# Adding the experts' rows to two DRAM buffers in turn, with a third buffer for results

## Chip, cores and metric

One core of a Trainium2 chip. The metric is the device time of one launch, in microseconds; the kernel before takes 2149.32 us (median of 3 runs, 2149.24 to 2149.33).

## What is computed

Two transformer blocks on 512 tokens of width 1024, in float32. The first block ends in a mixture of experts, and the change lies there and in the step behind it:

```python
def moe_ffn(h, ...):
    ...
    def expert_block(acc, blk):
        tok, wts, e = blk
        out = swiglu(h_pad[tok], w_gu[e], w_down[e])
        return acc.at[tok].add(out * wts[:, None].astype(out.dtype)), None
    acc, _ = lax.scan(expert_block, jnp.zeros((N + 1, D), h.dtype), ...)
    return acc[:N] + swiglu(h, w_sh_gu, w_sh_down)
...
        x_lat = x_lat + gt2 * rms_norm(f_lat.reshape(B, T, D), g_post_ffn[l])
```

There are 64 experts of inner width 256; each token goes to 8 of them, and its 8 weighted results are summed. To this comes a shared expert for all tokens. The second block begins with a norm of the sum.

## The kernel before

Everything runs on one core. The program is written in order, with tiles taken from pools; each tile has a tag, and a tag has a number of buffers. Outside stretches marked otherwise, a list scheduler that works at compile time, with its own estimates of each instruction's time, orders the instructions of each engine, and waits on semaphores keep the dependences. With another dependence it can find another order. An engine works through its queue in order, so an instruction that waits holds up everything behind it.

**The expert stage** (`experts`, from L1206 on) goes over groups of one or two experts. For each group it

- gathers the rows of the group's tokens from `h2d` in DRAM (`gather`, on POOL's queue) and turns them with PE (`expert_rows`);
- loads the expert's weights, 3 MB, through SP's queue into `raw` buffers and splits each piece into a high part on ACT (L132, `whi`) and a low part on DVE (L133, `wlo`), so that three products on PE make one in float32;
- forms the first product and the gate (`expert_in`; small blocks pass through a tile `esum`, L1044, with two buffers);
- one group later forms the second product (`expert_out`): ACT scales it into a result tile `ey` of 128 x 1024 (L1071), a tag with two buffers.

The result is then summed into the tokens' rows in two ways. The first 384 columns (`CA`) go through PE: ACT and POOL split them into `eys` (L1084, L1085), DVE makes a one-hot matrix (L1087), and PE adds the product to four accumulators `acc` (L1094). The other 640 columns go through DRAM: `expert_send` (L1075) issues an indirect DMA on POOL's queue that adds the rows to the buffer `cb` in DRAM. Since such an addition reads and writes `cb`, each one waits until the one before it has landed. It also reads `ey`, so a buffer of `ey` comes free only when its addition has landed. `cb` is cleared at the start by four DMAs on SP's queue (L1219). A loop at the end, for experts with more tokens than planned for, sends to `cb` too.

With two parts in a group there are 67 additions. `finish` puts an addition behind the subtraction L1085 of its group (`issue_after`) if that is the group's last expert.

**The combination** (`second_block`, L1435 on) starts when PE has added the shared expert to `acc` and to four more PSUM tiles. SP loads the four tiles of `cb` into `cf` (L1455, L1459) and the four of `x1d` into `cx` (L1456, L1461). Here DVE, ACT and POOL are under `manual_schedule`: they keep the order of the program. `take` copies PSUM to SBUF on ACT (L1469 to L1471); `add` (L1474) adds the two, for tile 0 on DVE and for tiles 1 to 3 on POOL; `squares` (L1477) sums squares on ACT. Tile 0 then goes ahead alone: norm, residual, next norm, turned by PE (L1392) and split again by ACT and DVE. DVE does the `rstd` of tiles 1 to 3 (one call, 128x3) after tile 0's normed row and before tile 0's split:

```python
                for t in range(2, NT):
                    squares(fs[t], ss[:, t:t + 1])
                rs = self.rstd(wp, ss[:, 1:], D)
                self.turn_tile(pp, xn, xs[0], xs[1], 0)
```

Then come the products of the second block, which need the split.

Of the kernel before, what the change touches and what calls it, by code (L numbers as in the profile page):

```python
# [1 line left out]

# [8 lines left out]
F = mybir.dt.float32  # L11
R = mybir.dt.float32r
# [9 lines left out]
T = 512  # L22
# [43 lines left out]
class Kernel:  # L66
# [762 lines left out]
    def order(self, mp, pp):  # L829


        nc, r = self.nc, self.route
        MM, key = r["MM"], r["key"]
        ka, kb, kac, kbc = key[:, 0:64], key[:, 64:128], key[:, 128:129], key[:, 129:130]
        ps = pp.tile([128, 65], F, tag="mm", name="mm", bufs=4)
        for t in range(NT):
            nc.tensor.matmul(ps[:, 0:64], r["ones"], MM[:, t, 0], start=t == 0, stop=t == NT - 1)
        for t in range(NT):
            nc.tensor.matmul(ps[:, 64:65], MM[:, t].rearrange("p a e -> p (a e)"), r["ones"][:, 0:1], start=t == 0, stop=t == NT - 1)
        tl = lambda name, *s: mp.tile([128, *s], F, name=name)  # L840
        v = nc.vector
        row, col, gt, rank = tl("krow", 64), tl("kcol", 1), tl("kgt", 64), tl("krank", 1)
        v.tensor_mul(row, ps[:, 0:64], ka)
        v.tensor_add(row, row, kb)
        v.tensor_scalar(col, ps[:, 64:65], kac, kbc, op0=OP.mult, op1=OP.add)
        v.tensor_scalar(gt, row, col, None, op0=OP.is_gt)
        v.tensor_reduce(rank, gt, axis=X, op=OP.add)
        perm = r["perm"]
        for i in range(2):
            h = slice(64 * i, 64 * i + 64)  # L850
            v.tensor_scalar(perm[h, h], self.iota_f[h, 0:64], rank[h], None, op0=OP.is_equal)

        p2 = pp.tile([128, NT, 128], F, tag="mm", name="tp", bufs=4)
        for t in range(NT):
            nc.tensor.transpose(p2[:, t], r["MW"][:, t].rearrange("p a e -> p (a e)"), self.ident)
        mt = mp.tile([128, D], F, tag="ey", name="kmt", bufs=2)[:, 0:512].rearrange("p (t e) -> p t e", t=NT)
        nc.scalar.activation(mt, p2, AF.Copy)
        ps = pp.tile([128, 64], F, tag="mm", name="mm", bufs=4)
        nc.tensor.matmul(ps, key[0:64, 130:258], perm[0:64, 0:64], start=True, stop=True)
        v.tensor_copy(r["eid"], ps)  # L860
        v.tensor_copy(r["eidi"], r["eid"])
        ps = pp.tile([128, NT, 2, 64], F, tag="mm", name="mm", bufs=4)
        for t in range(NT):
            nc.tensor.matmul(ps[:, t].rearrange("p a e -> p (a e)"), mt[:, t], perm, start=True, stop=True)
        M = mp.tile([128, NT, 64], BF, name="kM")
        v.tensor_copy(M, ps[:, :, 0])
        w = r["MW"][:, :, 1]
        nc.scalar.activation(w, ps[:, :, 1], AF.Copy)
        self.three_parts(v, r["aux"], w)
        self.places(pp, M, r["pos"])  # L870
        ps = pp.tile([128, 64], F, tag="mm", name="mm", bufs=4)
        for t in range(NT):
            nc.tensor.matmul(ps, r["ones"], M[:, t], start=t == 0, stop=t == NT - 1)
        v.tensor_copy(r["cnt"], ps)
# [110 lines left out]
    def expert_rows(self, tiles, pp, xg, parts=((0, 128),)):  # L985


        nc = self.nc
        pool, tags = tiles
        m = parts[-1][1]  # L990
        w = parts[0][1]
        if len(tags) == 2:
            hi, lo = (pool.tile([128, KD, 128], R, tag=tag, name="xT", bufs=2)[:, :, 0:m] for tag in tags)
            cut, out = [(lambda z: z, hi, lo)], [(hi, lo)]
        else:
            x = pool.tile([128, KD, 256], R, tag=tags[0], name="xT", bufs=2)
            if len(parts) == 1:
                at = 128 if w > 64 else w
                hi, lo = x[:, :, 0:w], x[:, :, at:at + w]
                cut, out = [(lambda z: z, hi, lo)], [(hi, lo) if w > 64 else (x[:, :, 0:2 * w],)]  # L1000
            elif w == 64:
                v = x.rearrange("p k (j h w) -> p k h j w", j=2, h=2)
                cut = [(lambda z: z.rearrange("p k (j w) -> p k j w", j=2), v[:, :, 0], v[:, :, 1])]
                out = [(x[:, :, 0:128],), (x[:, :, 128:256],)]
            else:

                cut = [(lambda z: z[:, :, 0:w], x[:, :, 0:w], x[:, :, 256 - w:256]),
                       (lambda z: z[:, :, w:m], x[:, :, w:m], x[:, :, m:256 - w])]
                out = [(x[:, :, 0:w], x[:, :, 256 - w:256]), (x[:, :, w:256 - w],)]
        for u in range(2):  # L1010
            p2 = pp.tile([128, 4, 128], F, tag="mm", name="tp", bufs=4)[:, :, 0:m]
            for k in range(4):
                c = (4 * u + k) * 128
                nc.tensor.transpose(p2[:, k], xg[0:m, c:c + 128], self.ident[0:m, 0:m])
            for some, hi, lo in cut:
                self.split_ps(hi[:, 4 * u:4 * u + 4], lo[:, 4 * u:4 * u + 4], some(p2))
        return out

    def expert_in(self, mp, pp, gu, blocks, between=None):
# [17 lines left out]
        for ps, (xT, a, p0, p1) in zip(pss, blocks):  # L1037
            if len(xT) == 2:
                nc.scalar.activation(a[p0:p1], ps[p0:p1, 0:256], AF.Silu)
                nc.vector.tensor_mul(a[p0:p1], a[p0:p1], ps[p0:p1, 256:512])  # L1040
            else:

                n = p1 - p0
                s = mp.tile([128, 512], F, tag="esum", name="esum", bufs=2)[p0:p1]  # L1044
                nc.scalar.activation(s, ps[n:2 * n], AF.Copy)
                nc.vector.tensor_add(s, ps[0:n], s)  # L1046
                nc.scalar.activation(a[p0:p1], s[:, 0:256], AF.Silu)
                nc.vector.tensor_mul(a[p0:p1], a[p0:p1], s[:, 256:512])
# [74 lines left out]
    def first_block(self):  # L1123

        nc, tc, ins = self.nc, self.tc, self.ins
        dram = lambda name, n, m=D: self.dram.tile([n, m], F, name=name)
        h2d, x1d, cb = dram("h2d", T), dram("x1d", T), dram("cb", T, D - CA)
        self.g3d = dram("g3d", 1)
        rctx, hctx = ExitStack(), ExitStack()
        yT, rows = self.mixer(rctx)  # L1130
# [75 lines left out]
    def experts(self, mp, pp, h2d, cb, acc, shared, gT, sums, grow, ahead, extra):  # L1206
# [8 lines left out]

        room(mp, AHEAD)
        free = xgs[:]
        for t in range(NT):
            nc.sync.dma_start(cb[t * 128:(t + 1) * 128, :], xgs[-1][:, 0:D - CA])  # L1219
        gu = lambda e: ins["w_expert_gu"][e]  # L1220
        dn = lambda e: ins["w_expert_down"][e]
        groups = self.plan()
# [69 lines left out]
        for g in range(len(groups) + 1):  # L1292
# [3 lines left out]
            def advance():  # L1296

                if late:
                    lg, a, nums = late
                    aT = [self.expert_turn(more, pp, x) for x in a]  # L1300
                    y.extend(mp.tile([128, D], F, tag="ey", name="ey", bufs=2) for _ in a)
                    for j, e in enumerate(nums):
                        outs.append((e, [(b, aT[b], tabs[rows_of[lg][b]][1], y[b], p0, p1)
                                         for b, parts in enumerate(groups[lg][1]) for i, p0, p1, _ in parts if i == j]))
# [5 lines left out]
            def finish():  # L1310
# [12 lines left out]
                with tc.issue_after(last.ins) if last else ExitStack():  # L1323
                    for b, _, _, y_, p0, p1 in parts:
                        i = rows_of[lg][b]
                        gi = tabs[i][3][[p[1] for p in groups[lg][1][b]].index(p0)]
                        self.expert_send(y_, gi, p0, p1, cb)

            if g < len(groups):
                es, bs = groups[g]  # L1330
# [19 lines left out]
        with tc.If(total > 0):  # L1350
            cnt = xp.tile([128, 1], F, name="xcnt")
            nc.vector.memset(cnt, 0.0)
            with tc.For_i(0, total):
# [3 lines left out]
                self.gather(gi, xgs[0], h2d)  # L1357
                a = mp.tile([128, 256], F, tag="eact", name="act", bufs=4)
                self.expert_in(mp, pp, gu(ev), [(self.expert_rows(tiles, pp, xgs[0])[0], a, 0, 128)])
                y = mp.tile([128, D], F, tag="ey", name="ey", bufs=2)  # L1360
                self.expert_out(pp, dn(ev), [(self.expert_turn(more, pp, a), wt, y, 0, 128)])
                self.expert_add(acc, *self.expert_parts(mp, y, row)[0])
                self.expert_send(y, gi, 0, 128, cb)
                nc.vector.tensor_scalar(cnt, cnt, 1.0, None, op0=OP.add)

        rest = []
# [68 lines left out]
    def second_block(self, x1d, cb, acc, more, release):  # L1435
# [9 lines left out]
        vr = vctx.enter_context(right("b2v")).tile([128, NT, D], F, name="rv")  # L1445
        with right("comb") as wp, ExitStack() as wctx:
            fs = [wp.tile([128, D], F, name=f"cf{t}") for t in range(NT)]
            sh = [wp.tile([128, D - CA], F, name=f"csh{t}") for t in range(NT)]
            sq = wp.tile([128, D], F, name="csq")
            g3 = wp.tile([128, D], F, name="g3")  # L1450
# [1 line left out]
            x1 = [wp.tile([128, D], F, name=f"cx{t}") for t in range(NT)]  # L1452
            ss = wp.tile([128, NT], F, name="css")
            rows = [slice(t * 128, (t + 1) * 128) for t in range(NT)]
            nc.sync.dma_start(fs[0][:, CA:], cb[rows[0], :])  # L1455
            nc.sync.dma_start(x1[0], x1d[rows[0], :])  # L1456
            gain = self.bc_rows(ins["norm_mix_gain_2"], D, "gmix", wp)
            for t in range(1, NT):
                nc.sync.dma_start(fs[t][:, CA:], cb[rows[t], :])  # L1459
            for t in range(1, NT):  # L1460
                nc.sync.dma_start(x1[t], x1d[rows[t], :])  # L1461
            units = self.each_unit(wctx, self.quarters("w_v_2"), self.first_raws, [None, None, None, nc.gpsimd])
# [1 line left out]
            with tc.manual_schedule(engines={ET.DVE, ET.Activation, ET.Pool}):  # L1464
# [6 lines left out]
                    nc.scalar.activation(sh[t][:, 512 - CA:], more[t], AF.Copy)  # L1471

                def add(t, e):
                    e.tensor_add(fs[t][:, CA:], fs[t][:, CA:], sh[t])  # L1474

                def squares(x, ss):
# [7 lines left out]
                squares(fs[0], ss[:, 0:1])  # L1484
                nc.vector.tensor_mul(y, fs[0], g3)
                self.scale_add(x1[0], y, self.rstd(wp, ss[:, 0:1], D), x1[0])
                add(1, nc.gpsimd)
                squares(fs[1], ss[:, 1:2])
                take(3)
                add(2, nc.gpsimd)  # L1490
                add(3, nc.gpsimd)
                release()
                pp = ctx.enter_context(tc.tile_pool(name="b2ps", bufs=1, space=PSUM))
# [503 lines left out]
```

## Time and profile before

| | |
|---|---|
| median of 3 runs | 2149.32 us |
| the profiled execution, its own time | 2145.43 us |
| its span | 2143.7 us |
| mean granted TensorE clock | 0.975 |
| PE busy | 2003.4 us, 93% of the span |
| DVE busy | 1444.8 us, 67% |
| ACT busy | 1094.4 us, 51% |
| POOL busy | 538.4 us, 25% |
| moved by DMA | 386.63 MB, mean 180 GB/s |

PE is TensorE, DVE VectorE, ACT ScalarE, POOL GpSimd, SP the engine that issues most DMAs. Busy time is the time in which an engine executes instructions; what it waits for between them is inferred from semaphores. The granted clock is a share of full speed, 2.4 GHz; the other level is 1.2 GHz, 0.5. In a timeline a row gives start, duration, engine, line, operation, what is written and read, and in brackets the idle time just before with what ended it. All times count from the start of the span.

### The profile page before, as it was taken

Reading aid. Unit: us, or ns where it says so; the run is one execution under the profiler, and the core shown is the slowest. Engines: PE = TensorE matmul, PEld = TensorE weight load, DVE = VectorE, ACT = ScalarE, POOL = GpSimd, SP = SyncE. Lnnn points to the kernel's source line nnn. Section 1 sums busy time; section 2 is a strip of 40 time slices with the busy share of each in tenths; the row PEclk is TensorE's granted clock in tenths of the full one; section 3 lists DMA queues with packets and bytes.
Section 4 is the critical chain, followed back from the end, with each engine's and each line's share of the span. In section 5 each row is a group of like instructions: output and inputs, shape, how many; then the busy total and the mean of one; then the engine's idle time right before and its main releaser. Section 6 shows DMA issues by size and latency. Waiting matters only on the chain. (4 is left out here: it accounts for less than half of the span.)

```text
span 2143.7 us, 27459 instructions
## 1 busy us (share of the span) xinstructions
PE 2003.4 (93%) x10031; PEld 1610.5 (75%) x10031; DVE 1444.8 (67%) x2495; ACT 1094.4 (51%) x1620; POOL 538.4 (25%) x307
## 2 busy tenths in 40 slices
PE   7999999998898899899889896999999999999998
PEld 4878888877876676667766674777788878888886
DVE  6667767648898898899889896556853345333344
ACT  7445433233387688789778785334232224232232
POOL 0322231011245365445544232111100001010110
PEclk9999999999899999999999998999999999999999
DMA  7111136633499889899888896421122232222221
GB/s 296 68 40 60 41 126 248 239 122 143 172 333 324 283 305 324 287 347 339 289 326 305 301 325 215 146 74 60 40 89 99 98 128 108 98 99 98 99 79 40
DMA packets 69710, 386.63 MB, mean 180 GB/s; under 512 B 11374, under 2 KB 12351, under 8 KB 30020
## 3 DMA queue, kind: packets, MB, share of 16 engines
q1 hardware_dynamic: 56932, 357.56, 45.4%
q0 software_dynamic: 12640, 27.29, 5.1%
q8 instruction: 80, 1.31, 0.2%
q14 instruction: 58, 0.48, 0.1%
HBM read 369.99 MB, written 23.55 MB: 184 GB/s over the span
## 5 line engine op out<-in xcount | busy, mean ns | idle before, releaser
L133 DVE TENSOR_TENSOR wlo<-raw,whi 128x1024 fp32r<-128x1024 f32 x586 | 720.2, 1256 | 216.0 <-ACT whi L132 211.4
L132 ACT ACTIVATE whi<-raw 128x1024 fp32r<-128x1024 f32 x592 | 607.3, 1055 | 331.3 <-PE mm L147 191.7
L1075 POOL DMA_INDIRECT cb<-ey,sgi x67 | 165.2, 2466 | 257.3 <-ACT ey L1071 112.6
L146 PE MATMUL mm<-hT,whi 128*128 128x512 f32 x320 | 127.6, 399 | 0.0
L147 PE MATMUL mm<-hT,whi 128*128 128x512 f32 x320 | 126.4, 396 | 0.0
L148 PE MATMUL mm<-hT,wlo 128*128 128x512 f32 x320 | 126.0, 394 | 0.0
L147 PE MATMUL mm<-x,whi 128*128 128x512 f32 x304 | 122.5, 403 | 0.0
L1602 POOL TENSOR_TENSOR relu<-relu 128x512 f32<-128x512 f32 x32 | 42.9, 1341 | 315.0 <-ACT relu L1600 315.0
L146 PE MATMUL mm<-x,whi 128*128 128x512 f32 x304 | 120.9, 398 | 0.0
L148 PE MATMUL mm<-x,wlo 128*128 128x512 f32 x304 | 120.8, 397 | 0.0
L1033 PE MATMUL mm<-wlo,xT 128*128 128x512 f32 (+1 forms) x280 | 115.8, 414 | 4.2 <-DVE wlo L133 4.1
L1033 PE MATMUL mm<-whi,xT 128*128 128x512 f32 (+1 forms) x280 | 114.4, 409 | 1.9 <-ACT whi L132 1.6
L1094 PE MATMUL acc<-eys,eoh 128*128 128x384 f32 (+2 forms) x376 | 88.3, 357 | 28.6 <-POOL eys L1085 26.9
L146 PE MATMUL mm<-whi,xT 128*96 128x512 f32 (+1 forms) x256 | 107.3, 419 | 5.3 <-DVE esum L1046 5.1
L147 PE MATMUL mm<-wlo,xT 128*96 128x512 f32 (+1 forms) x256 | 104.2, 407 | 3.5 <-DVE wlo L133 3.4
L147 PE MATMUL mm<-wlo,eaT 128*128 128x512 f32 (+2 forms) x268 | 106.9, 401 | 0.7 <-DVE wlo L133 0.5
L981 POOL DMA_INDIRECT xg<-h2d,sgi x47 | 87.6, 1864 | 76.9 <-issue 26.2
L1071 ACT ACTIVATE ey<-mm,swt 64x512 f32<-64x512 f32 (+3 forms) x134 | 88.5, 680 | 34.4 <-DMA cb<-ey,sgi 19.9
L1085 POOL TENSOR_TENSOR eys<-ey,eys 128x384 fp32r<-128x384 f32 (+2 forms) x47 | 82.5, 1757 | 92.9 <-ACT eys L1084 79.6
L146 PE MATMUL mm<-whi,eaT 128*128 128x512 f32 (+2 forms) x268 | 102.0, 398 | 3.8 <-ACT eaT L152 1.7
L148 PE MATMUL mm<-whi,eaT 128*128 128x512 f32 (+2 forms) x268 | 105.2, 395 | 0.0
L146 PE MATMUL mm<-y,whi 128*128 128x512 f32 (+2 forms) x272 | 103.2, 379 | 0.0
(542 smaller groups left out, 4761.4 us busy)
## 6 DMA issues: line engine op xcount, KB each, us to landing
raw<-in_w_expert_gu SPq DMA_DIRECT2D x128, 1024.0 KB, 7.4
raw<-in_w_expert_down SPq DMA_DIRECT2D x64, 1024.0 KB, 7.4
raw<-in_w_in SPq DMA_DIRECT2D x41, 1024.0 KB, 4.9
raw<-in_w_ff SPq DMA_DIRECT2D x32, 1024.0 KB, 4.9
raw<-in_w_ada SPq DMA_DIRECT2D x24, 1024.0 KB, 7.1
raw<-in_w_out SPq DMA_DIRECT2D x8, 1024.0 KB, 5.4
raw<-in_w_v SPq DMA_DIRECT2D x4, 1024.0 KB, 5.1
raw<-in_w_ret_up SPq DMA_DIRECT2D x4, 1024.0 KB, 4.7
```

The source lines that it names most:

```text
L132: nc.scalar.activation(hi, rv[:, k:k + n], AF.Copy)
L133: (engine or nc.vector).tensor_sub(lo, rv[:, k:k + n], hi.bitcast(F))
L146: mm(ps, ah, bh, start=start, stop=False)
L147: mm(ps, ah, bl, start=False, stop=False)
L148: mm(ps, al, bh, start=False, stop=stop)
L981: self.nc.gpsimd.indirect_dma_start(out=xg[0:gi.shape[0]], out_offset=None, in_=h2d, in_offset=bass.IndirectOffsetOnAxis(ap=gi, axis=0), b ...
L1033: nc.tensor.matmul(ps[0:xT[0].shape[2]], xT[0][:, kk], z[:, k], start=kk == i == 0, stop=kk == KD - 1 and i == 1)
L1071: nc.scalar.activation(y[p0:p1, sl], ps[p0:p1], AF.Copy, scale=wt[p0:p1])
L1075: self.nc.gpsimd.indirect_dma_start(out=cb, out_offset=bass.IndirectOffsetOnAxis(ap=gi, axis=0), in_=y[p0:p1, CA:], in_offset=None, bounds ...
L1085: last = nc.gpsimd.tensor_sub(yl, y[0:m, :CA], yh.bitcast(F))
L1094: self.nc.tensor.matmul(acc[t][:, 0:CA], oh[:, t * 128:(t + 1) * 128], y, start=False, stop=False)
L1602: nc.gpsimd.tensor_mul(sq, r, r)
```

## The change

Rows are added to two buffers in DRAM, `cb0` and `cb1`, in turn: an addition now waits for the last but one. Both are cleared. `ey` gets three buffers, and so do the other tiles of its tag; `esum` goes from two to one. In the combination the second buffer's tile is loaded into one more SBUF tile, `cg`, which has a single buffer, so the load for the next 128 tokens waits until the tile before has been read; `add` becomes two additions.

```diff
-            hi, lo = (pool.tile([128, KD, 128], R, tag=tag, name="xT", bufs=2)[:, :, 0:m] for tag in tags)
+            hi, lo = (pool.tile([128, KD, 128], R, tag=tag, name="xT", bufs=3)[:, :, 0:m] for tag in tags)
...
-                s = mp.tile([128, 512], F, tag="esum", name="esum", bufs=2)[p0:p1]
+                s = mp.tile([128, 512], F, tag="esum", name="esum", bufs=1)[p0:p1]
...
-        h2d, x1d, cb = dram("h2d", T), dram("x1d", T), dram("cb", T, D - CA)
+        h2d, x1d = dram("h2d", T), dram("x1d", T)
+
+        cb = [dram(f"cb{i}", T, D - CA) for i in range(2)]
...
-        for t in range(NT):
-            nc.sync.dma_start(cb[t * 128:(t + 1) * 128, :], xgs[-1][:, 0:D - CA])
+        for c in cb:
+            for t in range(NT):
+                nc.sync.dma_start(c[t * 128:(t + 1) * 128, :], xgs[-1][:, 0:D - CA])
+        sent = itertools.cycle(cb)
...
-                    y.extend(mp.tile([128, D], F, tag="ey", name="ey", bufs=2) for _ in a)
+                    y.extend(mp.tile([128, D], F, tag="ey", name="ey", bufs=3) for _ in a)
...
-                        self.expert_send(y_, gi, p0, p1, cb)
+                        self.expert_send(y_, gi, p0, p1, next(sent))
...
-                self.expert_send(y, gi, 0, 128, cb)
+                self.expert_send(y, gi, 0, 128, cb[0])
...
             fs = [wp.tile([128, D], F, name=f"cf{t}") for t in range(NT)]
+            f2 = []
+
+            def second(t):
+
+                f2.append(wp.tile([128, D - CA], F, tag="cg", name="cg"))
+                nc.sync.dma_start(f2[t], cb[1][rows[t], :])
...
-            nc.sync.dma_start(fs[0][:, CA:], cb[rows[0], :])
+            nc.sync.dma_start(fs[0][:, CA:], cb[0][rows[0], :])
+            second(0)
             nc.sync.dma_start(x1[0], x1d[rows[0], :])
             gain = self.bc_rows(ins["norm_mix_gain_2"], D, "gmix", wp)
             for t in range(1, NT):
-                nc.sync.dma_start(fs[t][:, CA:], cb[rows[t], :])
+                nc.sync.dma_start(fs[t][:, CA:], cb[0][rows[t], :])
...
                 def add(t, e):
+                    e.tensor_add(sh[t], sh[t], f2[t])
                     e.tensor_add(fs[t][:, CA:], fs[t][:, CA:], sh[t])
...
                 self.scale_add(x1[0], y, self.rstd(wp, ss[:, 0:1], D), x1[0])
+                second(1)
                 add(1, nc.gpsimd)
                 squares(fs[1], ss[:, 1:2])
                 take(3)
+                second(2)
                 add(2, nc.gpsimd)
+                second(3)
                 add(3, nc.gpsimd)
```

## Rows read from the trace of the kernel before

**Rows 1.** Windows: start to end, length, busy us (instructions) per engine, granted clock, DMA.

```profile
600.00:1306.00 706.00, 647.49 (x3203) 489.62 (x3202) 632.02 (x940) 571.35 (x806) 319.44 (x153) 0.97 0.89 312
1306.00:1420.00 114.00, 92.89 (x397) 74.46 (x396) 56.53 (x95) 39.18 (x63) 22.97 (x13) 0.90 0.44 157
```

**Rows 2.** Waits, 600 to 1306 us: waiter <- waited for, total us, times, longest.

```profile
POOL cb L1075 <- DMA cb<-ey,sgi: 75.0, 18, 8.8
...
PE acc L1094 <- POOL eys L1085: 26.9, 15, 8.1
...
ACT ey L1071 <- DMA cb<-ey,sgi: 19.9, 6, 6.8
```

**Rows 3.** Timeline of ACT, expert stage: two waits before `ey`.

```profile
731.41 0.68 ACT L1071 ACTIVATE ey<-mm,swt 64x512 f32<-64x512 f32 x1 [6.82 <-DMA cb<-ey,sgi]
...
1215.84 0.68 ACT L1071 ACTIVATE ey<-mm,swt 64x512 f32<-64x512 f32 x1 [5.04 <-DMA cb<-ey,sgi]
```

**Rows 4.** Timeline of PE, expert stage: stalls with the chains spoken of.

```profile
741.07 0.74 PE L146 MATMUL mm<-whi,xT 128*96 128x512 f32 x1 [5.08 <-DVE esum L1046]
...
806.42 1.14 PE L1094 MATMUL acc<-eys,eoh 128*128 128x384 f32 x5 [1.42 <-POOL eys L1085]
...
871.63 1.01 PE L1094 MATMUL acc<-eys,eoh 96*128 96x384 f32 x2 [8.05 <-POOL eys L1085]
...
1032.54 2.61 PE L1094 MATMUL acc<-eys,eoh 128*128 128x384 f32 x7 [5.26 <-POOL eys L1085]
...
1083.40 1.33 PE L1094 MATMUL acc<-eys,eoh 96*128 96x384 f32 x3 [3.21 <-POOL eys L1085]
...
1217.52 0.50 PE L1033 MATMUL mm<-whi,xT 128*128 128x512 f32 x1 [1.57 <-ACT whi L132]
```

**Rows 5.** DMA issues: tensor, queue, count, KB each, median us to landing.

```profile
cb<-xg SPq DMA_DIRECT2D x4, 320.0 KB, 2.4
...
cb<-ey,sgi POOLq DMA_INDIRECT x67, 7.8
```

**Rows 6.** Timelines of DVE and POOL, around 687 and 861 us.

```profile
685.37 6.89 DVE L133 TENSOR_TENSOR wlo<-raw,whi 128x1024 fp32r<-128x1024 f32 x6
...
687.32 5.79 POOL L1085 TENSOR_TENSOR eys<-ey,eys 96x384 fp32r<-96x384 f32 x1 [4.48 <-ACT eys L1084]
...
861.12 6.89 DVE L133 TENSOR_TENSOR wlo<-raw,whi 128x1024 fp32r<-128x1024 f32 x6
...
860.05 9.18 POOL L1075 DMA_INDIRECT cb<-ey,sgi  x1 [4.69 <-DVE eoh L1087]
...
870.57 1.01 POOL L1085 TENSOR_TENSOR eys<-ey,eys 96x384 fp32r<-96x384 f32 x1
```

**Rows 7.** Windows behind four stalls, columns as in rows 1.

```profile
741.00:750.00 9.00, 8.93 (x35) 6.20 (x36) 7.23 (x25) 4.78 (x7) 3.39 (x3) 0.78 0.87 268
871.60:880.00 8.40, 8.37 (x31) 6.92 (x32) 3.50 (x6) 4.38 (x7) 1.45 (x1) 0.81 0.41 114
1032.60:1042.00 9.40, 9.40 (x37) 8.14 (x38) 4.20 (x6) 4.30 (x7) 2.80 (x2) 0.68 0.49 132
1083.50:1092.00 8.50, 8.03 (x24) 6.29 (x24) 3.06 (x5) 2.79 (x4) 2.53 (x2) 0.63 0.84 301
```

**Rows 8.** Timeline of SP: the clearing of `cb`.

```profile
547.62 2.00 SPq L1219 DMA_DIRECT2D cb<-xg  x4
```

**Rows 9.** Timelines of ACT, DVE and POOL in the combination.

```profile
1315.61 0.49 ACT L1469 ACTIVATE cf<-acc 128x384 f32<-128x384 f32 x1 [11.80 <-PE mm L148]
...
1320.90 0.82 DVE L1474 TENSOR_TENSOR cf<-cf,csh 128x640 f32<-128x640 f32 x1 [14.08 <-DMA cf<-cb]
...
1325.24 6.07 POOL L1474 TENSOR_TENSOR cf<-cf,csh 128x640 f32<-128x640 f32 x3 [17.11 <-DMA cf<-cb]
...
1333.12 0.16 DVE L177 TENSOR_SCALAR rsx<-css 128x3 f32<-128x3 f32 x1
```

**Rows 10.** DMA rate from 1300 to 1345 us, in 40 slices of 1.125 us.

```profile
GB/s 58 248 393 301 80 255 422 371 364 374 157 18 0 0 44 269 218 388 410 360 340 395 434 422 411 408 310 26 7 0 0 0 0 0 0 0 386 80 138 415
```

More of the change, by code (lines that the diff above doesn't have):

```diff
@@ L1 @@
+import itertools
 from contextlib import ExitStack
@@ L855, in order @@
             nc.tensor.transpose(p2[:, t], r["MW"][:, t].rearrange("p a e -> p (a e)"), self.ident)
-        mt = mp.tile([128, D], F, tag="ey", name="kmt", bufs=2)[:, 0:512].rearrange("p (t e) -> p t e", t=NT)
+        mt = mp.tile([128, D], F, tag="ey", name="kmt", bufs=3)[:, 0:512].rearrange("p (t e) -> p t e", t=NT)
         nc.scalar.activation(mt, p2, AF.Copy)
@@ L1359, in experts @@
                 self.expert_in(mp, pp, gu(ev), [(self.expert_rows(tiles, pp, xgs[0])[0], a, 0, 128)])
-                y = mp.tile([128, D], F, tag="ey", name="ey", bufs=2)
+                y = mp.tile([128, D], F, tag="ey", name="ey", bufs=3)
                 self.expert_out(pp, dn(ev), [(self.expert_turn(more, pp, a), wt, y, 0, 128)])
                 self.expert_add(acc, *self.expert_parts(mp, y, row)[0])
-                self.expert_send(y, gi, 0, 128, cb)
+                self.expert_send(y, gi, 0, 128, cb[0])
                 nc.vector.tensor_scalar(cnt, cnt, 1.0, None, op0=OP.add)
```

## The prediction

> **What bounds the kernel now.** I read the windows by stage first. The expert stage (600 to 1306 us) keeps PE busy for 647.49 of 706 us and DVE for 632.02, at a mean granted clock of 0.97; in the stretch behind it, which holds the combination, PE works 92.89 of 114 us [rows 1]. So in the expert stage PE stands still for 58.5 us, with DVE close behind it: besides clock this is all that the change can reach there.
>
> Then the waits of the expert stage [rows 2]. POOL waits 75.0 us, 18 times, for an earlier addition of rows to land (`cb<-ey`), since every addition writes the same buffer. ACT waits 19.9 us, 6 times, for the same landings: it wants to write a result tile `ey` whose two buffers are both still being read. PE waits 26.9 us, 15 times, at the sums `acc` for the subtraction `eys` on POOL. POOL is not the bound, but this subtraction stands behind additions in its queue, so their waits can reach PE.
>
> **Third `ey` buffer.** I looked up what ACT's two longest waits of this kind do to PE: 6.82 us before 731.41 and 5.04 us before 1215.84 [rows 3]. Shortly after each, PE stands still: 5.08 us before 741.07 (for `esum`, which DVE made late because ACT had been late) and 1.57 us before 1217.52 [rows 4]. With a third buffer, the tile that ACT asks for was read by an addition one further back, so these waits go. I take 5.08 + 1.57 = 6.7 us off. Ends: 0, if DVE's weight splits `wlo` are late next (DVE is busy 632 of 706 us), and 19.9, all of ACT's waits. `esum` loses its second buffer. It lives from ACT's copy to DVE's product and there is at most one per expert, 706/64 = 11 us apart; this distance hides the loss, and I cost it at nothing. Were it gone, ACT would wait there as it now does for `ey`.
>
> **Two buffers in turn.** There are 67 additions in 706 us, 10.5 us apart on the mean, and one lands after 7.8 us in the median [rows 5]. An addition that waits for the last but one has some 21 us, so POOL's 75 us go almost wholly. Behind a waiting addition on POOL stand gathers and the subtraction. PE's four long waits with such a chain are 1.42 + 8.05 + 5.26 + 3.21 = 17.9 us [rows 4]; that is the upper end. But look at the longest. The addition began at 860.05, took 9.18 us, and ended about a microsecond after DVE's run of six `wlo` subtractions, 861.12 to 868.01; the subtraction that PE needed began at 870.57 [rows 6]. With no wait POOL would have come to it earlier, inside the same DVE run, and another one shows what happens there: at 687.32 it took 5.79 us with nothing ahead of it, ending 0.9 us behind such a DVE run, 685.37 to 692.26 [rows 6]. So it would have ended near 869.0 instead of 871.6, and PE would have got back 2.6 of its 8.05 us, a third. A third of 17.9 is 6 us, what I hold for nearly sure if the order stays; 0 is the lower end, if a new order puts another subtraction into a DVE run. I take 9, between 6 and the middle of 6 and 17.9, because not every subtraction meets such a run.
>
> The Trainium skill states this as a rule (SBUF — State Buffer, "Who interferes with whom"): a VectorE instruction with two SBUF inputs and a GpSimd instruction that reads SBUF shut each other out, the later one for as long as the other runs. The subtraction at 687.32 agrees [rows 6].
>
> **Clock.** Behind the stalls at 741, 871, 1032 and 1083 the mean granted clock is 0.78, 0.81, 0.68 and 0.63 over 9, 8.4, 9.4 and 8.5 us, that is, PE spends a part of them at 1.2 instead of 2.4 GHz [rows 7]. The work lost is 0.22 x 9 + 0.19 x 8.4 + 0.32 x 9.4 + 0.37 x 8.5 = 9.7 us. It comes back only where a stall goes or becomes short: I take half, 5 us; ends 0 and 9.7.
>
> Expert stage: 6.7 + 9 + 5 = 20.7 us less.
>
> **Order.** Outside the combination a list scheduler orders each engine's work by its own estimates, so other dependences give another order everywhere in the stage. The trace has no price for that. The nearest rows are PE's stalls themselves, 1.4 to 8.05 us each [rows 4]: one long one more or fewer is 8 us either way. I take 0 and keep 8 for the range.
>
> **Clearing the second buffer.** Four more writes of 320 KB; the present four take 2.00 us of SP's time from 547.62 and land after 2.4 us [rows 5, 8]. The additions begin only in the expert stage, 50 us later, and this time hides them: nothing. Were that cover gone, the next weight load would be 2 us later.
>
> **Combination.** This is the price, and it can be followed step by step, because DVE, ACT and POOL keep the order of the program there. The stage starts when PE ends the shared expert: ACT's first copy, at 1315.61, waits for PE, not for the last addition [rows 9], so an earlier last addition gains nothing. The loads then run at 340 to 434 GB/s until about 1330 [rows 10]. DVE adds tile 0 at 1320.90, 0.82 us; the change puts a second such add ahead of it and one load more among those it waits for (320 KB, 0.8 us at 400 GB/s): 1.6 us, beside which the following chain runs. That chain is the single buffer `cg`. The load for tile 1 is issued only when DVE has read tile 0's, about 1323, behind all the loads that SP has issued, so it lands when these are through, about 1330. POOL's additions for tiles 1 to 3, which now begin at 1325.24 and take 6.07 us, 2.0 each [rows 9], become six. For tiles 2 and 3 the load waits for POOL's first add, takes 2.4 us and an estimated 0.3 for issue, while the second add of 2.0 runs beside it: a period of 4.7 us. The last add ends at 1330 + 4.7 + 4.7 + 4.0 = 1343.4, against 1331.3, which is 12.1 us later. The `rstd` of tiles 1 to 3 (`rsx`, 128x3) began at 1333.12 [rows 9], 1.8 us behind POOL's last add, and stands in DVE's queue ahead of the split of tile 0 that PE's next product needs. So this `rstd`, and PE's restart with it, comes 12.1 us later. Ends: 8.1 (loads through by 1326) and 17.5 (one of the loads lands after 7.8 us, as an addition does, instead of 2.4). SP's stores and weight loads behind the waiting loads move along with PE.
>
> **Sum.** 20.7 - 12.1 = 8.6 us less. The profiled execution took 2145.43 us (1.7 more than its span of 2143.7), so 2136.8 for it; the median of the runs, 2149.32, is 3.9 above that execution, which I carry over: 2140.7 us.
>
> **Rivals.**
> 1. *Slower: the single `cg` buffer.* The new wait is the chain of load and add for tiles 1 to 3, at 1320 to 1345 us. It decides as soon as the expert stage gives back less than it costs. At 17.5 us for it and only 6.7 back for `ey`, the time is 2149.3 + 10.8 = 2160.1. For it: every step of the chain is forced by the order. Against: the stalls behind additions are there to be won. Chance 0.26.
> 2. *No change: DVE keeps POOL.* Additions no longer wait for each other, but subtractions still come out when DVE's runs end. Then 6.7 + 6 + 2 (the clock behind the first stall) = 14.7 come back, less 12.1: 2146.7. For it: both DVE runs [rows 6]. Against: it supposes that every one of these subtractions meets a run. The rule of the skill above says no more than that those which meet one wait. Chance 0.24.
> 3. *Faster still:* 6.7 + 17.9 + 9.7 - 12.1 = 22.2 less, 2127.1. Against: DVE, at 632 us, would be busy for 94% of what is left of the stage. Chance 0.14.
> 4. *The turn does nothing for PE,* because the new order uses the buffers without moving the subtractions: that leaves `ey` and the price, the loss of rival 1, and is counted there.
>
> **How the numbers follow.** A measurement here tells about 0.2%, 4.3 us, from no change. My forecast has 0.36; with rival 3 that is 0.50 for faster, 0.24 for no change (rival 2), 0.26 for slower (rival 1). The range reaches from rival 3, with 6 of the order's 8 us, 2121, to rival 1, 2160. The forecast's own range is 2132 to 2145.
>
> **What would show it.** Right: POOL's waits on `cb<-ey` down to a few us in all; none of ACT's before `ey`; PE's waits for `eys` down from 26.9 to some 17 us; the `rstd` of tiles 1 to 3 some 30 us behind ACT's first copy of the combination instead of 17.5; six adds on POOL, spaced by loads of `cg`. Wrong: PE still idle for near 58 us in the expert stage with the clock at 0.97 (rivals 1 and 2); or a price under 8 us in the combination because the load for tile 1 lands before 1326.

## The result, and the profile after

The kernel after takes 2124.01 us (median of 4 runs, 2119.46 to 2125.86), before on the same chip 2149.32 (4 runs): 25.3 us less, ratio 0.9878 with an interval of 0.9860 to 0.9895. The direction of the forecast held, its size did not: 8.6 us was forecast.

The profiled execution took 2125.86 us, its span is 2124.2. Against the profiled execution of before (2145.43) that is 19.6 less. So 5.7 of the 25.3 us are how the two profiled executions stand to their medians, and the parts below are made against the 19.5 us between the two spans.

Each span is cut at two events: the first addition to `cb`, and ACT's first copy of the combination. The windows between the two, of before and after (columns as in [rows 1]):

```profile
604.30:1315.61 711.31, 652.90 (x3215) 493.87 (x3215) 628.54 (x936) 567.21 (x801) 319.84 (x152) 0.97 0.88 310
```

```profile
605.25:1282.77 677.52, 643.45 (x3215) 488.25 (x3215) 619.50 (x936) 567.13 (x800) 318.36 (x152) 0.99 0.92 326
```

The expert stage is 33.8 us shorter. PE runs the same 3215 instructions in 643.45 instead of 652.90 us (9.5 less; the granted clock, 0.99 instead of 0.97, is most of it: by the clock records of the two traces PE loses 6.8 instead of 14.8 us of work to the lower level) and stands still for 34.1 instead of 58.4 us (24.3 less). All that follows the first copy takes 2124.2 - 1282.77 = 841.4 instead of 828.1 us, 13.3 more. The first addition starts 0.95 us later. Sum: -33.8 + 13.3 + 0.95 = -19.5.

The waits of this stretch after the change, with columns as in [rows 2]:

```profile
POOL cb L1076 <- ACT ey L1072: 142.7, 19, 14.7
...
PE acc L1095 <- POOL eys L1086: 13.6, 11, 6.4
...
PE tp L1057 <- DVE act L1049: 1.8, 4, 0.8
```

No wait for an addition to land is left, neither POOL's 75.0 us nor ACT's 19.9 [rows 2]; what POOL's additions wait for now is ACT, which writes their rows (142.7 us, 112.6 before). PE's waits for the subtraction are halved. PE's timeline of after has four stalls of over 1.2 us left, where before had twelve, six of them in [rows 4]:

```profile
696.01 0.69 PE L1095 MATMUL acc<-eys,eoh 96*128 96x384 f32 x1 [2.79 <-POOL eys L1086]
...
858.82 1.01 PE L1095 MATMUL acc<-eys,eoh 96*128 96x384 f32 x2 [6.39 <-POOL eys L1086]
...
1111.17 0.45 PE L1095 MATMUL acc<-eys,eoh 96*128 96x384 f32 x1 [1.21 <-POOL eys L1086]
...
1264.16 0.62 PE L1095 MATMUL acc<-eys,eoh 128*128 128x384 f32 x2 [1.53 <-ACT eys L1085]
```

The stalls at 741, 806, 1032, 1083 and 1217 of [rows 4] have no successor of over 0.3 us. The one at 871.63 is now at 858.82 and lost 1.66 of its 8.05 us. In the expert stage the engines run the instructions of before in the order of before, so none of this comes from another order. The same holds for all kernels below but sub_dve, so that one stall can be followed from kernel to kernel.

The combination of after, in the timelines of ACT, SP, POOL, DVE and PE:

```profile
1282.77 0.49 ACT L1483 ACTIVATE cf<-acc 128x384 f32<-128x384 f32 x1 [10.86 <-PE mm L149]
...
1290.34 0.32 SPq L1458 DMA_DIRECT2D cg<-cb  x1
...
1301.23 5.02 SPq L1458 DMA_DIRECT2D cg<-cb  x2
...
1299.68 1.53 POOL L1488 TENSOR_TENSOR csh<-csh,cg 128x640 f32<-128x640 f32 x1 [28.59 <-DMA xd<-cx]
1301.29 1.53 POOL L1489 TENSOR_TENSOR cf<-cf,csh 128x640 f32<-128x640 f32 x1
1304.37 1.53 POOL L1488 TENSOR_TENSOR csh<-csh,cg 128x640 f32<-128x640 f32 x1 [1.56 <-DMA cg<-cb]
...
1309.05 1.76 POOL L1488 TENSOR_TENSOR csh<-csh,cg 128x640 f32<-128x640 f32 x1 [1.54 <-DMA cg<-cb]
1310.89 1.53 POOL L1489 TENSOR_TENSOR cf<-cf,csh 128x640 f32<-128x640 f32 x1
...
1313.63 0.17 DVE L178 TENSOR_SCALAR rsx<-css 128x3 f32<-128x3 f32 x1 [4.22 <-ACT csq L1492]
...
1309.72 1.94 PE L1397 MATMUL tp<-ident,xn 128*128 128x128 f32 x8 [27.11 <-issue]
1314.14 0.80 PE L147 MATMUL mm<-whi,x 128*128 128x512 f32 x1 [2.47 <-ACT x L153]
```

The `rstd` of tiles 1 to 3 begins 30.9 us behind ACT's first copy instead of 17.5 [rows 9]: 13.4 us later, as the 13.3 of the whole. POOL's pairs of additions start 4.69 and 4.68 us apart, the second and the third held by a load of `cg`. (For the first the profile names a store; what it needs is the load issued at 1290.34.)

### The profile page after: what moved, and what is told of

The parts are those of the page before. It is cut to its first block, busy times and chain, and to the rows that moved or that the text cites. A ratio compares the mean times of both kernels' runs of the same rounds, so it can differ in the third digit from the quotient of the medians.

```text
span 2124.2 us, 27476 instructions
## 1 busy us (share of the span) xinstructions
PE 1994.3 (94%) x10031; PEld 1603.2 (75%) x10031; DVE 1435.1 (68%) x2496; ACT 1093.8 (51%) x1620; POOL 541.1 (25%) x310
## 5 line engine op out<-in xcount | busy, mean ns | idle before, releaser
L1076 POOL DMA_INDIRECT cb<-ey,sgi x67 | 150.0, 2238 | 161.8 <-ACT ey L1072 142.7
L1086 POOL TENSOR_TENSOR eys<-ey,eys 128x384 fp32r<-128x384 f32 (+2 forms) x47 | 103.3, 2198 | 129.7 <-ACT eys L1085 129.5
L147 PE MATMUL mm<-y,whi 128*128 128x512 f32 (+2 forms) x272 | 103.2, 379 | 0.0
L149 PE MATMUL mm<-y,wlo 128*128 128x512 f32 (+2 forms) x272 | 103.1, 379 | 0.0
L148 PE MATMUL mm<-y,whi 128*128 128x512 f32 (+2 forms) x272 | 103.1, 379 | 0.0
L982 POOL DMA_INDIRECT xg<-h2d,sgi x47 | 77.9, 1657 | 99.0 <-PE tp L1015 27.8
```

Of the source, the lines that this page charges most:

```text
L147: mm(ps, ah, bh, start=start, stop=False)
L148: mm(ps, ah, bl, start=False, stop=False)
L149: mm(ps, al, bh, start=False, stop=stop)
L982: self.nc.gpsimd.indirect_dma_start(out=xg[0:gi.shape[0]], out_offset=None, in_=h2d, in_offset=bass.IndirectOffsetOnAxis(ap=gi, axis=0), b ...
L1076: self.nc.gpsimd.indirect_dma_start(out=cb, out_offset=bass.IndirectOffsetOnAxis(ap=gi, axis=0), in_=y[p0:p1, CA:], in_offset=None, bounds ...
L1086: last = nc.gpsimd.tensor_sub(yl, y[0:m, :CA], yh.bitcast(F))
```

## The experiments

All compare with runs of the kernel before on the same chip (medians 2146.28, 2146.89, 2148.47 and 2148.49 us in the four groups of runs). The spans of the profiled executions are cut as above; "behind" is from ACT's first copy to the end, and PE's idle and busy time is that in the stage.

| kernel | turn | `ey` | stage | PE idle | PE busy | behind |
|---|---|---|---|---|---|---|
| before | no | 2 | 711.3 | 58.4 | 652.9 | 828.1 |
| tail_only | no | 2 | 715.7 | 60.1 | 655.6 | 841.0 |
| ey_only | no | 3 | 697.5 | 48.9 | 648.5 | 828.8 |
| turn_only | yes | 2 | 681.6 | 38.9 | 642.8 | 840.9 |
| xn_turn, xn_turn_b | yes | 2 | 681.3, 680.2 | 38.6, 36.7 | 642.8, 643.5 | 832.8, 833.0 |
| after | yes | 3 | 677.5 | 34.1 | 643.5 | 841.4 |
| xn_slots, xn_slots_b | yes | 3 | 673.8, 673.5 | 33.2, 32.8 | 640.6, 640.7 | 833.1, 832.8 |
| xn_slots_rs | yes | 3 | 675.8 | 35.3 | 640.5 | 836.0 |
| xn_ahead | yes | 3 | 673.4 | 32.9 | 640.6 | 838.2 |
| xn_dve | yes | 3 | 673.7 | 33.4 | 640.3 | 834.1 |
| sub_dve | yes | 3 | 684.5 | 38.0 | 646.5 | 839.0 |

**tail_only: the second buffer without its use.** From the kernel after, everything but the turn and the numbers of buffers:

```diff
-                        self.expert_send(y_, gi, p0, p1, next(sent))
+                        self.expert_send(y_, gi, p0, p1, cb[0])
```

with `ey` at two and `esum` at two buffers again. Expected:

> Kernel before, with the second buffer cleared, loaded through the single cg buffer and added in the combination, but all additions of rows still sent to the first buffer, and two ey buffers. My theory (the combination costs 13 us, as the two traces read side by side: from ACT's first copy to the rstd of tiles 1 to 3 it is 30.8 us in the changed kernel and 17.5 before): 2149.3 + 13 = 2162 us. Rival (a part of those 13 us is work that the shorter expert stage pushed into it): under 2157 us.

Measured: 2158.23 us (10 runs), ratio 1.0055 (1.0037 to 1.0073), 12.0 us more by the medians (11.8 by the ratio). Behind the first copy it takes 841.0 us, 12.9 more than before. From the 2146.28 us of the same chip the theory asks 2159.3 and the rival less than 2154, so the theory holds: the price of the combination was rightly found and sized.

**ey_only: the third buffer without the turn.** From the kernel before, `bufs=3` for `ey` and the tiles of its tag, `bufs=1` for `esum`. Expected:

> Kernel before with three ey buffers and one esum buffer, one buffer in DRAM. If waits simply add up: stalls of 5.08 + 1.57 and three small ones of 2.1 in all, with 2 us of clock, are gone: 2138.5 us. Rival (the wait that ACT loses, POOL has instead, since an earlier result only meets an addition that has not landed): 2145 to 2150 us. By either, the two parts and the combination sum to about 15 us less than before, 10 short of the 25 measured, if they do not help one another.

Measured: 2133.41 us (10 runs), ratio 0.9943 (0.9923 to 0.9962), 12.9 us less by the medians (12.2 by the ratio). That is about what the theory asks (10.8 less) and not the rival. ACT waits for no addition any more; the stalls of 8.05, 5.26 and 3.21 us before the subtraction stand as they were. PE's waits for `act` (1.79 us at 775.28 in before) and `oh` (1.43 at 791.00) fall to 0.34 and 0.11, and the one at 806 grows to 4.28.

**turn_only: the turn without the third buffer.** From the kernel after, `bufs=2` for `ey` and `esum`. Expected:

> Two buffers in turn, but two ey buffers and two esum buffers as before. If waits simply add up: PE's stalls behind additions that are gone or shorter in the changed kernel, 1.42 + 5.26 + 3.21 + 1.7 = 11.6, with the clock behind two of them, 6.1, are 17.7 us less, and the combination is 13 more: about 2145 us. Rival (additions without waits are worth little as long as ACT must wait for an ey buffer): 2155 to 2162 us.

Measured: 2124.81 us (4 runs), ratio 0.9891 (0.9862 to 0.9920), 21.5 us less by the medians (23.4 by the ratio, as the expectations below have it), with the combination's 12 us already paid. Both theories missed, and this miss places the error: the turn alone shortens the stage by about 32 us (29.7 against before, 34.1 against tail_only, which differs from it by the turn alone), and not by the 9 for it and a share of the clock's 5. PE's idle time falls by 19.5 us, from 58.4 to 38.9. Of PE's stalls in [rows 4] only `esum` (5.05 us) and the rest of the longest one (6.39) remain. ACT still waits for landed additions, 7.3 us in 2 waits, where before had 19.9 in 6.

**xn_slots: the same, with the second buffer's tiles loaded early.** Tiles 1 and 2 go to buffers of another tag (`xn`) that is not yet in use, tile 3 to `cg` as soon as DVE has read tile 0's:

```diff
-                f2.append(wp.tile([128, D - CA], F, tag="cg", name="cg"))
+                if t in (1, 2):
+                    f2.append(wp.tile([128, D], F, tag="xn", name="cgx", bufs=2)[:, 0:D - CA])
+                else:
+                    f2.append(wp.tile([128, D - CA], F, tag="cg", name="cg"))
...
                 nc.sync.dma_start(fs[t][:, CA:], cb[0][rows[t], :])
+                if t < 3:
+                    second(t)
...
                 add(0, nc.vector)
+                second(3)
...
-                second(1)
...
-                second(2)
...
-                second(3)
```

> Changed kernel with the second buffer's loads for tiles 1 and 2 put into the two buffers of xn, which are free until then, and issued among the other loads; tile 3's load into cg right after tile 0's add. My theory (the combination's price is the chain of load and add through one buffer): POOL's six adds then follow each other without load between them, the rstd of tiles 1 to 3 comes some 9 us earlier, 2115 us. Rival (the loads are bound by the DMA rate, so all that is gained is in the last two loads): 2119 us or more.

Measured: 2111.51 us (4 runs), ratio 0.9839 (0.9810 to 0.9868), 34.8 us less than before. It beats both kernels. Behind the first copy it takes 833.1 us instead of 841.4, and the `rstd` of tiles 1 to 3 comes 24.2 us behind that copy instead of 30.9, so the theory holds, at 6.7 us and not 9. The other 3.7 us lie in the expert stage (673.8 instead of 677.5), which the edit does not touch; what brought them no run shows. The same kernel was run once more:

> The same kernel as xn_slots, run again beside the next two so that they can be compared on one chip: 2111 to 2115 us, 33 to 35 us less than before.

2111.72 us, ratio 0.9833 (0.9815 to 0.9852).

**xn_turn: xn_slots without the third buffer**, run twice. Expected:

> The kernel after with the second buffer's tiles loaded early (as in xn_slots, 2111.5 us), but ey with two buffers and esum with two, so only the turn is left of the expert stage's part of the change. Theory 1, the two parts of the change free the same waits (the turn alone gave the stage 23.4 + 11.8 = some 35 us, both together 25.3 + 11.8 = 37): the third ey buffer is worth 1 to 4 us on top of the turn, so 2112 to 2116 us. Theory 2, the prediction's sum, in which the two add up: without 6.7 us for ey and its clock, some 2120 us or more; by what the third buffer gave alone (12.2 us) it would be 2124.

> The same kernel as xn_turn (ey and esum with two buffers each), run again beside xn_slots to size the third ey buffer on top of the turn. Theory 1, the third buffer still takes away waits of ACT that the turn leaves (7.3 us, 2 times, in the run with the turn alone): 4 to 7 us over xn_slots. Theory 2, the turn has freed them already: within 3 us of xn_slots.

Measured: 2118.35 us, ratio 0.9870 (0.9843 to 0.9896), and, on one chip with xn_slots_b, 2117.51 us, ratio 0.9861 (0.9839 to 0.9884): 5.8 us over xn_slots_b. The first lies between the two theories, the second in the 4 to 7 us of theory 1. The table says the same: with the turn, the stage takes 681.0 us on the mean of three without the third buffer and 674.6 of six with it, leaving sub_dve out. So the third buffer is worth 6.4 us on top of the turn (4.1 from turn_only to after, 6.7 among the xn kernels). Alone it gave 16 us of the stage (713.5, the mean of two, to 697.5), and the turn alone 32.5. The two don't add up (48.5 against 38.9 for both): additions that start sooner also free `ey` sooner (ACT's waits above), and PE's waits of 1.79, 1.43 and 1.57 us at 775, 791 and 1217 go with either part alone, so they count only once.

**sub_dve: the subtraction on DVE.** From the kernel after; the edit also frees the additions from their place behind the subtraction, and other instructions move too, since the scheduler finds another order:

```diff
-        last = nc.gpsimd.tensor_sub(yl, y[0:m, :CA], yh.bitcast(F))
+        last = nc.vector.tensor_sub(yl, y[0:m, :CA], yh.bitcast(F))
...
-                with tc.issue_after(last.ins) if last else ExitStack():
+                with ExitStack():
```

> The kernel after (2124.0 us) with the subtraction for eys on DVE instead of POOL, behind nothing of POOL's queue. Another order of the instructions comes with it, so lengths of stalls are told by sums only. Theory 1, what is left of PE's waits for POOL's subtraction (13.6 us in all, 6.4 the longest) comes from DVE's runs holding POOL: with the subtraction on DVE itself those waits go and the stage gets up to 13 us shorter, 2111 to 2118 us. Theory 2, DVE is the next bound: it is busy for 620 of 677 us, 67 subtractions more at half a microsecond make it 650, and the time gets longer, 2128 us or more.

Measured: 2127.44 us (4 runs), ratio 0.9903 (0.9878 to 0.9928); after had 0.9878 (0.9860 to 0.9895). No gain. PE's waits in the stage, columns as in [rows 2]:

```profile
PE mm L148 <- DVE wlo L134: 7.9, 13, 1.3
PE mm L1034 <- DVE wlo L134: 4.6, 5, 2.2
PE tp L1057 <- DVE act L1049: 3.9, 5, 1.3
PE tp L1015 <- ACT ey L1072: 3.5, 3, 2.2
```

The waits for POOL are gone, and DVE and ACT are late in their place: PE stands still for 38.0 us, not 34.1. Theory 2 has the time nearly right but not its reason: the trace has 47 subtractions, not 67, and DVE is busy for 624.5 instead of 619.5 us, not 650. What is left of the waits for POOL's subtraction was not had by giving it to DVE. With the other order and the freed additions, this says nothing on single stalls.

**Three ways to restart PE sooner**, all from xn_slots, where PE begins with tile 0 24.5 us behind ACT's first copy. xn_slots_rs moves the `rstd` of tiles 1 to 3 behind the turn and split of tile 0:

```diff
-                rs = self.rstd(wp, ss[:, 1:], D)
                 self.turn_tile(pp, xn, xs[0], xs[1], 0)
+                rs = self.rstd(wp, ss[:, 1:], D)
```

> xn_slots (2111.5 us) with the rstd of tiles 1 to 3 moved behind tile 0's turn and split in the program, so that tile 0's split no longer stands behind POOL's six additions in DVE's queue. Theory 1, PE's restart hangs on that rstd alone: PE gets tile 0 some 10 us sooner, and the time falls by 5 to 10 us, to 2102 to 2106, as the products for tile 0 alone then run beside the additions. Theory 2, PE wants tiles 1 to 3 right after tile 0, so it waits there instead: the same time within 3 us, 2109 to 2114.

Measured: 2116.40 us (4 runs), ratio 0.9862 (0.9842 to 0.9882), neither theory's time; behind the first copy 836.0 us, 3 more than xn_slots, and 2 more in the stage, where PE waits 2.06 us at the stall of 1083 again. PE got tile 0 no sooner (24.3 us), as this `rstd` stands behind the normed row that PE turns; what seemed to hold that row were ACT's squares for tile 0, behind those of tile 1. Tile 1 came later. xn_ahead therefore puts these squares ahead of those of tile 1, and tile 0's split ahead of the other tiles' squares:

```diff
                 self.scale_add(x1[0], y, self.rstd(wp, ss[:, 0:1], D), x1[0])
+                ss0 = wp.tile([128, 1], F, name="css0")
+                squares(x1[0], ss0)
...
                 nc.vector.tensor_scalar(xn, y, self.rstd(wp, ss0, D), None, op0=OP.mult)
+                self.turn_tile(pp, xn, xs[0], xs[1], 0)
                 for t in range(2, NT):
                     squares(fs[t], ss[:, t:t + 1])
                 rs = self.rstd(wp, ss[:, 1:], D)
-                self.turn_tile(pp, xn, xs[0], xs[1], 0)
```

> xn_slots with ACT's order changed for tile 0: the squares for its second norm stand ahead of the squares of tile 1, which wait for POOL's sum, and its turn and split stand ahead of the squares and the rstd of the other tiles. Theory 1, tile 0 is held by ACT's queue alone (in xn_slots ACT's squares of cx came at 1294.82 although DVE had cx at 1288.9): PE gets tile 0 some 6 to 7 us earlier, and the time falls by 4 to 7 us against xn_slots. Theory 2, the products for tile 0 are held by the weights' splits or by tile 1 a moment later: within 2 us of xn_slots.

Measured: 2118.22 us (4 runs), ratio 0.9858 (0.9837 to 0.9879), 6.5 us slower than xn_slots_b beside it. Both theories fell. The squares came early, and then DVE's chain for tile 0 ran into POOL's additions. DVE and POOL of xn_ahead:

```profile
1295.35 1.12 DVE L182 SCALAR_TENSOR_TENSOR rsz<-rsy,rsx 128x1 f32<-128x1 f32 x1
...
1296.70 1.38 DVE L182 SCALAR_TENSOR_TENSOR rsz<-rsy,rsx 128x1 f32<-128x1 f32 x1
1298.11 1.46 DVE L186 SCALAR_TENSOR_TENSOR rsy<-rsz,rsy 128x1 f32<-128x1 f32 x1
1299.61 1.57 DVE L182 SCALAR_TENSOR_TENSOR rsz<-rsy,rsx 128x1 f32<-128x1 f32 x1
...
1296.53 1.53 POOL L1494 TENSOR_TENSOR cf<-cf,csh 128x640 f32<-128x640 f32 x1
1298.03 1.52 POOL L1493 TENSOR_TENSOR csh<-csh,cg 128x640 f32<-128x640 f32 x1
1299.63 1.53 POOL L1494 TENSOR_TENSOR cf<-cf,csh 128x640 f32<-128x640 f32 x1
```

Steps on one number a row, 0.16 to 0.22 us elsewhere, last until the addition on POOL beside them is done: the last three end at 1298.08, 1299.57 and 1301.18, the additions at 1298.06, 1299.55 and 1301.16. Tile 0 came only 0.8 us sooner than in xn_slots (23.7 behind the first copy), and tiles 1 to 3 later, since their squares now stood behind it. xn_dve, lastly, gives all additions to DVE, so that POOL runs nothing beside it:

```diff
-                add(1, nc.gpsimd)
+                add(1, nc.vector)
```

and the same for tiles 2 and 3.

> xn_slots (2111.5 and 2111.7 us, 34.7 and 36.8 less than before) with the additions of tiles 1 to 3 on DVE instead of POOL, so that nothing runs on POOL beside DVE's chain for tile 0. Theory 1, in the combination the two engines stretch each other (POOL's first additions took 2.3 to 2.6 us instead of 1.53, DVE's steps of rstd 0.96 and 1.38 instead of 0.22, its product of cy 2.44 instead of 1.22): six additions on DVE take 6 x 0.83 = 5 us, nothing is stretched, and PE starts tile 0 some 2 to 3 us earlier than 24.4 us behind ACT's first copy: 2108 to 2110 us. Theory 2, DVE then has the additions in its one queue ahead of tile 0's norm, and that costs what the stretching did: the same within 2 us, or up to 3 us more.

Measured: 2113.75 us (5 runs), ratio 0.9841 (0.9808 to 0.9874), not to be told from xn_slots (0.9833 and 0.9839), as theory 2 has it. Two of the six additions on DVE:

```profile
1290.28 0.82 DVE L1493 TENSOR_TENSOR csh<-csh,cgx 128x640 f32<-128x640 f32 x1
...
1295.40 0.83 DVE L1493 TENSOR_TENSOR csh<-csh,cg 128x640 f32<-128x640 f32 x1 [1.85 <-DMA cg<-cb]
```

Nothing is stretched, but six additions and a wait for a load now stand in DVE's one queue: PE gets tile 0 23.2 us behind the first copy, 1.3 sooner, and yet all that follows the first copy takes 1 us longer than in xn_slots.

## Why the prediction was right or wrong

**The step that failed is "Two buffers in turn"**: the sentence "So it would have ended near 869.0 ..., and PE would have got back 2.6 of its 8.05 us, a third. A third of 17.9 is 6 us", and the 9 taken from it. By itself the turn took 19.5 us off PE's idle time (turn_only), more than even the upper end of 17.9. For the stall that the third was read from, the size held: in after, POOL and DVE around that place are

```profile
850.22 7.52 POOL L982 DMA_INDIRECT xg<-h2d,sgi  x1 [3.68 <-PE tp L1015]
857.77 1.00 POOL L1086 TENSOR_TENSOR eys<-ey,eys 96x384 fp32r<-96x384 f32 x1
...
849.97 6.88 DVE L134 TENSOR_TENSOR wlo<-raw,whi 128x1024 fp32r<-128x1024 f32 x6
...
1001.09 7.67 POOL L1076 DMA_INDIRECT cb<-ey,sgi  x1 [4.65 <-ACT ey L1072]
1008.29 1.52 POOL L1086 TENSOR_TENSOR eys<-ey,eys 128x384 fp32r<-128x384 f32 x1
...
1049.45 4.12 POOL L982 DMA_INDIRECT xg<-h2d,sgi  x1 [1.54 <-DVE sgi L916]
1055.94 1.78 POOL L1086 TENSOR_TENSOR eys<-ey,eys 96x384 fp32r<-96x384 f32 x1 [2.38 <-ACT eys L1085]
...
1053.36 7.72 DVE L134 TENSOR_TENSOR wlo<-raw,whi 128x1024 fp32r<-128x1024 f32 x6
```

The gather at 850.22 meets DVE's run of six (not the subtraction itself, as the prediction had it), the subtraction follows at once, and only 1.66 us came back (2.6 were expected). But the other three stalls were not like it. These are their rows in before, with two more places that the prediction did not look at:

```profile
1028.25 3.21 POOL L1075 DMA_INDIRECT cb<-ey,sgi  x1 [5.61 <-DMA cb<-ey,sgi]
1030.98 1.50 POOL L1085 TENSOR_TENSOR eys<-ey,eys 128x384 fp32r<-128x384 f32 x1
...
1072.09 2.67 POOL L1075 DMA_INDIRECT cb<-ey,sgi  x1 [4.87 <-DMA cb<-ey,sgi]
1075.06 7.25 POOL L981 DMA_INDIRECT xg<-h2d,sgi  x1 [0.30 <-PE mm L148]
1082.35 1.00 POOL L1085 TENSOR_TENSOR eys<-ey,eys 96x384 fp32r<-96x384 f32 x1
...
1074.48 6.88 DVE L133 TENSOR_TENSOR wlo<-raw,whi 128x1024 fp32r<-128x1024 f32 x6
...
773.25 1.98 DVE L1048 TENSOR_TENSOR act<-act,esum 64x256 f32<-64x256 f32 x1 [0.18 <-ACT act L1047]
...
773.93 1.00 POOL L1085 TENSOR_TENSOR eys<-ey,eys 96x384 fp32r<-96x384 f32 x1
...
788.43 2.52 DVE L903 TENSOR_TENSOR oh<-riota,rpos 128x256 bf16<-128x256 f32 x2
...
788.81 1.50 POOL L1085 TENSOR_TENSOR eys<-ey,eys 128x384 fp32r<-128x384 f32 x1
...
775.28 0.44 PE L1056 MATMUL tp<-ident,act 128*128 128x128 f32 x2 [1.79 <-DVE act L1048]
...
791.00 0.35 PE L908 MATMUL tp<-raux,oh 128*128 128x6 bf16 x8 [1.43 <-DVE oh L903]
```

and DVE's rows at the last two places in after:

```profile
769.64 0.42 DVE L1049 TENSOR_TENSOR act<-act,esum 64x256 f32<-64x256 f32 x1 [0.17 <-ACT act L1048]
...
783.48 0.75 DVE L904 TENSOR_TENSOR oh<-riota,rpos 128x256 bf16<-128x256 f32 x2
```

- At 1032 the addition waited 5.61 us for an earlier one. Without that wait it runs at 1001.09 in after, and the subtraction is through before PE asks: all 5.26 us came back.
- At 1083 a gather was held inside a run of DVE, as the addition was at 871, but only because the addition ahead of it had waited 4.87 us. In after the gather runs beside the three splits that DVE has ahead of that run (1049.09 to 1052.57), and the subtraction gets into the run itself, 1.78 us, while the run takes 7.72 instead of 6.88: all 3.21 us came back.
- At 806 the 1.42 us came back too. So the four stalls gave 1.42 + 1.66 + 5.26 + 3.21 = 11.6 us, near the 9. "Inside the same DVE run" was true of one place and was carried to the others; a POOL that comes sooner also comes ahead of a run.
- The rest of the error has no term in the sum. By the overlap of the rows, a late subtraction of POOL also stretched DVE: the gate's product took 1.98 instead of 0.42 us beside one, and PE waited 1.79 for it; the two one-hot matrices 2.52 instead of 0.75, and PE waited 1.43. DVE's busy time for the same 936 instructions fell by 9.0 us in the stage. PE's waits for `act` and `oh` fell by 2.8 and 2.0 us; the third `ey` buffer alone takes these two waits away as well (ey_only), so they are not the turn's alone. Smaller waits for the subtraction gave 1.7 more.

**The clock** is the second term that was too small: "I take half, 5 us". PE's busy time for the same matmuls fell by 9.5 us, 8 of them by the clock records, almost the upper end: of the four stalls named three went altogether, and other stalls with them.

**Third `ey` buffer**: right in size. PE's idle time for `esum` and `whi`, the two named, fell by 4.8 and 2.0 us (6.7 expected). The stall for `esum` needed the buffer (5.05 us with the turn alone), the 1.57 us for `whi` at 1217 went with the turn alone too. On top of the turn the buffer was worth 6.4 us of the stage and 5.8 in time. That it gives some 12 us without the turn was not seen, as the two parts were treated as adding up. `esum`'s single buffer cost nothing that shows: PE waits 0.3 us for it in after.

**Order**: the 0 was right, its premise was not: the other dependences gave no other order, and that of the expert stage stayed. **Clearing**: the first addition came 0.95 us later, but at 601.6 to 605.3 in the kernels above that also clear two buffers, and at 602.15 in ey_only, which clears one: no cost can be told.

**Combination**: mechanism and size right, 13.3 against 12.1. The additions were faster than taken (1.53, not 2.0 us) and the first load landed later: POOL began 16.9 us behind ACT's first copy, not 14.4; that the period came out at 4.69 as worked out (4.7) is partly luck, since the addition in it was 0.5 us shorter than taken and the rest, from its end over the next load to the next addition, was 3.16 us and not 2.7. That the time for tile 0 itself hangs on this chain was not seen: ACT's squares for tile 0's second norm stand behind those of tile 1.

**Sum** on the profiled executions: stage -33.8 instead of -20.7, behind it +13.3 instead of +12.1, the start +0.95: -19.5 instead of -8.6. That is near rival 3 (22.2 less): the stalls and the clock came back but for the longest stall. That the number is so near is partly luck: of rival 3's 17.9 us only 11.6 came back, and waits that it did not count, 1.7 + 2.8 + 2.0 us, made up for the rest. Rival 1's chain was there, at the price of the forecast and not at 17.5; rival 2 named the one place where DVE does hold POOL, and took it for all.

## What to carry to other kernels

Follow every long stall to its own root before a share read from one of them is carried to the rest; the longest need not be typical. If an engine's waits make its instructions collide with a neighbour's, their removal also gives back what the neighbour lost and the clock behind each stall, so count these beside the waits. Load the second buffer of an accumulation early and into tiles of its own: that way the same change gave 35 us instead of 25, 8.3 of them in the combination.

## What was not expected of the hardware

- VectorE and GpSimd stretch each other by single instructions, and not only by whole runs: beside POOL's additions of 1.5 us, DVE steps of 0.16 to 0.22 us took 1.12 to 1.57. The Trainium skill (SBUF — State Buffer, "Who interferes with whom") says that a VectorE instruction with two SBUF inputs contends with a GpSimd instruction that reads SBUF, and that the port pair which the two share is an exclusive lock. The rows of xn_ahead agree: the last three steps end within 0.03 us of the additions. Rows of after show the lock to be held for single instructions: a waiting subtraction on POOL (1055.94, 1.78 us) got in between two of DVE's back-to-back subtractions, while the one at 687.32 in before took 5.79 us beside such a run [rows 6]. What decides between the two, no run shows.
- Gathers and additions issued by POOL are caught as well: the gather at 850.22 took 7.52 us beside a run of six subtractions on DVE, the one at 842.12 in the same trace 1.06, of which all but 0.3 lie ahead of DVE's next run. Which part of an issue is held, the rows don't show.
